# Attention of a two-block kernel: the softmax division moved from the probabilities to each head's output, with two units ahead

## The chip, the cores and the metric

The kernel runs on one core of one Trainium2 chip. The metric is the time of one execution in device microseconds (us); lower is better. The median of three runs stands for the kernel before.

## The reference, cut to what matters

Two transformer-like blocks work on one sequence of 1024 tokens of width 1024. The change lies in the attention of the second block: 8 heads of width 64, causal, with a bias of the distance and three dilated windows. Each branch is a softmax, and the three are merged by their softmax denominators:

```
for window, dilation in DILATED_BRANCHES:
    o, l = dilated_window_branch(q, k, v, slopes, window, dilation)
    ...
w = jax.nn.softmax(jnp.stack(lses, axis=-1), axis=-1)
o = jnp.einsum('bshn,nbshe->bshe', w, jnp.stack(outs, axis=0))
```

The merged branches equal one softmax over all keys, in which a key that lies in n branches counts n times. The kernel computes it so: the table `bias` of each head holds the distance term less log(n), and a large positive value where n is 0.

## The kernel before, in words

The kernel is one long program, traced by the class `Model`. Matrices are multiplied in two parts, a rounded high part and the rest (`hi`/`lo`, `wh`/`wl`, `ph`/`pl`), on TensorE. Tiles come from pools with a fixed number of buffers by tag: 32 buffers of 128x1024 floats with tag `u` (line 263), 5 of 128x512 for `tmp` (line 268), 8 PSUM banks (line 274), and 2 each of the tags `raw` and `xr` (line 305). Through `raw` go all weights on their way from DRAM: `fetch` (line 342) loads a piece into a `raw` buffer on SP's queue, ScalarE rounds it to `wh` (L351), GpSimd makes `wl` (L352); there are 5 buffers (`NW`) for the results, and a piece whose result has no buffer yet waits in `raw`.

Which instruction stands where in an engine's queue is not written by hand. Under `schedule_with_timeline_sim=True` a list scheduler goes through the traced program, simulates it with modelled durations and gives out buffers and places in the queues; among instructions that are ready the one earlier in the program goes first. On the chip each queue then runs in that fixed order.

The second block's mixer (`mixer2`, line 1655) makes q, k, v and u, runs the state-space part and its gate (`glu`, line 1507), and then `attention` (line 1634). What follows are four rounds of `down` (line 447) over the results of the gate and of the attention; each input is split by `hilo` (line 1499: ScalarE L1501, GpSimd L1504).

Attention goes through 8 heads in 4 pairs, and each head in 2 halves of 512 queries; a half is called a unit here, v0 to v15 in the order of the program. `heads_in` (line 1557) lays out the q and k of a pair: copies on ScalarE (L1565, L1566), subtractions on GpSimd (L1568, L1569), and DMAs on SP (L1567, L1570).

`softmax` (line 1582) takes a unit's 4 blocks of 128 queries. For each, TensorE makes the negated scores against all keys up to the block (L1601, L1602), VectorE adds the bias and takes the row minimum in one instruction (L1604), ScalarE makes the exponential in place and the row's sum, `den` (L1607), VectorE its reciprocal (L1608), and GpSimd multiplies the block of probabilities by it (L1609). A row is a partition here, so the reciprocal is one number a partition. An even unit (queries 0 to 511) has rows of 128 to 512 keys, an odd one of 640 to 1024.

`values` (line 1612) takes a unit's probabilities, 128 keys at a time: TensorE turns them (L1624), ScalarE rounds the result to `ph` (L1626), VectorE makes `pl` (L1627), and TensorE multiplies both by the head's values into the bank `po` (L1628, L1629). There queries run along the columns. At the end ScalarE copies one half of the bank to `vo` (L1631) and VectorE adds both halves into the pair's tile `at` (L1632).

`attention` keeps finished softmaxes in the list `late`. `values` of a unit is traced only after the softmax of the unit three later (line 1649).

Of the kernel before, what the change touches and what calls it, by code (L numbers as in the profile page):

```python
# [11 lines left out]
F32 = mybir.dt.float32  # L12
# [3 lines left out]
ALU = mybir.AluOpType  # L16
PSUM = bass.MemoryType.PSUM
DRAM = bass.MemoryType.DRAM
P = 128
# [3 lines left out]
H = 512  # L23
# [89 lines left out]
class Z:  # L113
# [3 lines left out]
    late = "s"  # L117
# [60 lines left out]
class ZS(Z):  # L178
# [4 lines left out]
    late = "u"  # L183
# [64 lines left out]
class Model:  # L248
# [1332 lines left out]

    def softmax(self, ops, bias, half):

        nc = self.nc
        qq, kd, kl = ops
        if half:
            ps = [self.u("P") for _ in range(4)]
        else:
            two = [self.u("P", shape=[P, 2, H]) for _ in range(2)]
            ps = [two[c // 2][:, c % 2] for c in range(4)]  # L1590
        mx, den = self.sm("mx", 8), self.sm("den", 4)
        for c, p in enumerate(ps):
            qb = 4 * half + c
            w = (qb + 1) * P
            o = 896 - qb * P
            cuts = [0, w] if w <= H else ([0, 384, w] if w < 896 else [0, H, w])
            init = 3.0e38
            for n, (k0, k1) in enumerate(zip(cuts, cuts[1:])):
                pp = self.bank()[:, : k1 - k0]
                qs = slice(qb * P, (qb + 1) * P)  # L1600
                nc.tensor.matmul(pp, qq[:, qs], kd[:, k0:k1], start=True, stop=False)  # L1601
                nc.tensor.matmul(pp, qq[:, qs], kl[:, k0:k1], start=False, stop=True)  # L1602
                m = mx[:, c : c + 1] if n == len(cuts) - 2 else mx[:, 4 + c : 5 + c]
                nc.vector.tensor_tensor_reduce(out=p[:, k0:k1], in0=pp, in1=bias[:, o + k0 : o + k1], scale=1.0,  # L1604
                                               scalar=init, op0=ALU.add, op1=ALU.min, accum_out=m)
                init = m
            nc.scalar.activation(p[:, :w], p[:, :w], AF.Exp, scale=-1.0, bias=mx[:, c : c + 1], accum_out=den[:, c : c + 1])  # L1607
            nc.vector.reciprocal(den[:, c : c + 1], den[:, c : c + 1])  # L1608
            nc.gpsimd.tensor_scalar(out=p[:, :w], in0=p[:, :w], scalar1=den[:, c : c + 1], scalar2=None, op0=ALU.mult)  # L1609
        return ps  # L1610

    def values(self, vv, a, ps, half, at):


        nc = self.nc
        po = self.bank("po")
        me, other = slice(64 * a, 64 * a + 64), slice(64 - 64 * a, 128 - 64 * a)
        last = 4 * half + 3
        for kt in range(last + 1):
            c0 = max(0, kt - 4 * half)  # L1620
            sl = slice(c0 * P, H)
            pp = self.bank()
            for c in range(c0, 4):
                nc.tensor.transpose(pp[:, c * P : (c + 1) * P], ps[c][:, kt * P : (kt + 1) * P], self.idn)  # L1624
            ph, pl = self.tmp("ph", dt=F32R), self.tmp("pl", dt=F32R)
            nc.scalar.activation(ph[:, sl], pp[:, sl], AF.Copy)  # L1626
            nc.vector.tensor_tensor(pl[:, sl], pp[:, sl], ph.bitcast(F32)[:, sl], op=ALU.subtract)  # L1627
            nc.tensor.matmul(po[:, sl], vv[:, kt, :], ph[:, sl], start=kt == 0, stop=False)  # L1628
            nc.tensor.matmul(po[:, sl], vv[:, kt, :], pl[:, sl], start=False, stop=kt == last)  # L1629
        t = self.tmp("vo")  # L1630
        nc.scalar.activation(t[me], po[other], AF.Copy)  # L1631
        nc.vector.tensor_tensor(at[me, half * H : half * H + H], po[me], t[me], op=ALU.add)  # L1632

    def attention(self, qk):

        at, late = [], []
        ops = [self.heads_in(*qk[0])]
        for j in range(4):
            at.append(self.u("at"))
            for a in range(2):  # L1640
                h = 2 * j + a
                bias = self.raw(self.a["bias"][h], name="bias", tag="xr")
                if a == 0 and j < 3:
                    ops.append(self.heads_in(*qk[j + 1]))
                vv = self.head_v(h)
                for half in range(2):
                    ps = self.softmax(ops[j][a], bias, half)
                    late.append((vv, a, ps, half, at[j]))
                    if len(late) > 3:
                        self.values(*late.pop(0))  # L1650
        while late:
            self.values(*late.pop(0))
        return [self.hilo(t) for t in at]
# [71 lines left out]
```

## Time and profile before

| | |
|---|---|
| median of 3 runs | 3072.33 us (3070.43 to 3072.90) |
| profiled execution, its own time | 3082.47 us |
| its span, first to last instruction | 3080.7 us |
| mean granted TensorE clock | 0.963 |
| busy, share of the span | TensorE 92%, VectorE 58%, ScalarE 43%, GpSimd 28% |
| chain that ended last | TensorE 62%, DMA 14%, VectorE 9%, ScalarE 6%, GpSimd 2% |
| attention in the span | about 2090 to 2270 us |

The profile shows one execution. PE is TensorE (PEld its weight loads), DVE VectorE, ACT ScalarE, POOL GpSimd and SP SyncE, which only issues DMAs here; L1609 is line 1609 of the kernel. Rows by line give busy time, mean ns of one, and the idle time of the engine just before them with what ended it. Rows in order of time give start and duration in us, and in brackets the idle time ahead. A release is inferred: with several waits it is the one that came last. Busy shares over the whole span are an average over stages with different limits.

### The profile page before, as it was taken

To read this page: it belongs to the slowest core of one execution; us is meant where nothing else is said; L and a number is where in the kernel's file an instruction comes from. 1 tells how busy PE (TensorE), PEld (TensorE's weight loads), DVE (VectorE), ACT (ScalarE), POOL (GpSimd) and SP (SyncE) were. 2 spreads that over 40 slices of the span, in tenths; PEclk is the share of its full clock that TensorE was granted. 3 is DMA by queue.
4 is the path that set the end of the run, shared out by engine and by line. 5 is a ranking of instruction groups with operands and counts; after the bars stand their busy time and mean duration, and the time that the engine had idled before them with its cause. 6 is when DMAs were issued, how large, how long until landed. Compare 5 with 4: busy or idle time off the path is not lost.

```text
span 3080.7 us, 33834 instructions
## 1 busy us (share of the span) xinstructions
PE 2821.6 (92%) x12585; PEld 2306.2 (75%) x12585; DVE 1775.9 (58%) x2527; ACT 1323.5 (43%) x1921; POOL 868.0 (28%) x667
## 2 busy tenths in 40 slices
PE   8998999898999979999978999997689899998998
PEld 7777788677777858777767778886677677776776
DVE  4576655487784365665667551417635756665445
ACT  5446555433445463333324452246644533333343
POOL 3331332211222432121111031459844212211002
PEclk9999999999999989999989999998899999999999
DMA  3114344564455123454466661523113244446556
GB/s 141 61 42 137 132 146 146 201 230 144 162 183 170 55 82 103 151 177 150 146 221 212 217 220 72 168 76 110 35 48 130 86 150 158 158 157 208 181 180 209
DMA packets 192309, 443.11 MB, mean 144 GB/s; under 512 B 23220, under 2 KB 23312, under 8 KB 192144
## 3 DMA queue, kind: packets, MB, share of 16 engines
q1 hardware_dynamic: 155600, 362.83, 35.4%
q10 hardware_dynamic: 36544, 78.13, 7.2%
q8 instruction: 98, 1.61, 0.2%
q14 instruction: 67, 0.55, 0.1%
HBM read 303.92 MB, written 131.60 MB: 141 GB/s over the span
## 4 chain that ended last, share of the span: by engine, by line
PE 62%; DMA 14%; DVE 9%; ACT 6%; issue 6%; POOL 2%; SPq 1%; ACTq 0%; DVEq 0%; POOLq 0%
PE b L541 22%; PE b L717 17%; PE b L455 4%; PE b L442 4%; DMA raw<-in_f_out 3%; DMA raw<-in_f_in 3%; DMA td<-tw 2%; DMA tw<-raw 2%; PE b L1103 2%; PE b L1101 2%; PE b L1102 2%; DMA sd<-hs 1%; ACT wh L481 1%; PE b L1624 1%; DVE wl L482 1%
## 5 line engine op out<-in xcount | busy, mean ns | idle before, releaser
L541 PE MATMUL b<-zh,wh 128*128 128x512 f32 x1680 | 644.9, 397 | 30.5 <-ACT wh L481 23.1
L541 PE MATMUL b<-zh,wl 128*128 128x512 f32 x1680 | 623.3, 392 | 8.4 <-DVE wl L482 3.3
L541 PE MATMUL b<-zl,wh 128*128 128x512 f32 x1560 | 612.8, 393 | 15.4 <-DVE zl L211 15.4
L717 PE MATMUL b<-tt,wh 128*128 128x512 f32 x1232 | 392.1, 400 | 51.8 <-ACT tt L698 46.5
L541 PEld LDWEIGHTS b<-zh,wh 128*128 128x128 f32 x1680 | 319.5, 190 | 117.2 <-ACT wh L481 35.1
L541 PEld LDWEIGHTS b<-zh,wl 128*128 128x128 f32 x1680 | 316.8, 189 | 78.6 <-DVE wl L482 4.6
L717 PE MATMUL b<-wl,wh 128*128 128x512 f32 x1344 | 323.5, 402 | 40.3 <-ACT wl L698 26.3
L541 PEld LDWEIGHTS b<-zl,wh 128*128 128x128 f32 x1560 | 295.4, 189 | 79.5 <-DVE zl L211 19.2
L717 PEld LDWEIGHTS b<-wl,wh 128*128 128x128 f32 x1344 | 258.7, 194 | 102.4 <-ACT wl L698 27.8
L717 PEld LDWEIGHTS b<-tt,wh 128*128 128x128 f32 x1232 | 237.5, 194 | 106.8 <-ACT tt L698 48.9
L482 POOL TENSOR_TENSOR wl<-raw,wh 128x1024 fp32r<-128x1024 f32 x60 | 148.0, 2469 | 392.4 <-ACT wh L481 368.9
L698 ACT ACTIVATE wh<-sd 128x1024 fp32r<-128x1024 f32 x140 | 141.7, 1014 | 254.3 <-PE b L717 127.0
L717 PE MATMUL b<-tt,wl 128*128 128x512 f32 x616 | 244.1, 397 | 0.0
L352 POOL TENSOR_TENSOR wl<-raw,wh 128x1024 fp32r<-128x1024 f32 (+1 forms) x58 | 142.6, 2464 | 305.0 <-ACT wh L351 274.1
L481 ACT ACTIVATE wh<-raw 128x1024 fp32r<-128x1024 f32 x120 | 126.8, 1059 | 226.0 <-DMA raw<-in_f_in 102.6
L383 POOL TENSOR_SCALAR v<-ss 128x1 f32<-128x1 f32 x80 | 46.4, 580 | 497.6 <-ACT junk L376 493.9
L618 POOL TENSOR_TENSOR hw<-h 128x512 f32<-128x512 f32 x38 | 59.2, 1558 | 409.2 <-DVE h L1188 173.2
L699 DVE TENSOR_TENSOR tt<-td,tt 128x1024 fp32r<-128x1024 f32 x84 | 95.2, 1134 | 115.4 <-ACT tt L698 115.2
L698 ACT ACTIVATE tt<-td 128x1024 fp32r<-128x1024 f32 x84 | 83.0, 988 | 162.7 <-DMA td<-tw 86.2
L699 DVE TENSOR_TENSOR wl<-sd,wh 128x1024 fp32r<-128x1024 f32 x84 | 97.4, 1159 | 77.1 <-ACT wh L698 77.1
L505 DVE TENSOR_TENSOR s<-raw 128x512 f32<-128x512 f32 x60 | 75.2, 1253 | 115.2 <-DMA raw<-in_f_in 105.2
L717 PEld LDWEIGHTS b<-tt,wl 128*128 128x128 f32 x616 | 119.1, 193 | 25.3
(362 smaller groups left out, 5301.0 us busy)
## 6 DMA issues: line engine op xcount, KB each, us to landing
sd<-hs SPq DMA_DIRECT2D x126, 512.0 KB, 4.0
raw<-in_f_in SPq DMA_DIRECT2D x94, 512.0 KB, 3.5
raw<-in_f_out SPq DMA_DIRECT2D x44, 512.0 KB, 3.6
tw<-raw SPq DMA_DIRECT2D x44, 512.0 KB, 2.9
wd<-in_w_down ACTq DMA_DIRECT2D x40, 512.0 KB, 8.9
td<-tw ACTq DMA_DIRECT2D x40, 512.0 KB, 4.3
hs<-h SPq DMA_DIRECT2D x38, 512.0 KB, 3.3
hs<-hw SPq DMA_DIRECT2D x38, 512.0 KB, 3.1
```

Source lines behind the costliest of these rows:

```text
L352: nc.gpsimd.tensor_tensor(l, r, h.bitcast(F32), op=ALU.subtract)
L442: nc.tensor.matmul(pp[n], w[:, k, :], z(m, k, slice(n * H, n * H + H)), start=k == 0 and w is wh and m == 0, stop=k == nk - 1 and w is wl)
L455: yield nc.tensor.matmul(pp, h[:, ts], w[:, sl], start=f == 0 and w is wh and h is hh, stop=f == len(hs) - 1 and h is hl)
L481: nc.scalar.activation(hi.rearrange("p a b -> p (a b)"), x, AF.Copy)
L482: eng.tensor_tensor(lo.rearrange("p a b -> p (a b)"), x, hi.bitcast(F32).rearrange("p a b -> p (a b)"), op=ALU.subtract)
L505: v.tensor_tensor(s1, a21, a22, op=ALU.add)
L541: self.mark = nc.tensor.matmul(bank, w, x, start=start and k == 0 and i == 0, stop=k == 3 and i == 2, skip_group_check=True)
L698: nc.scalar.activation(hi[:, :n], x[:, :n], AF.Copy)
L699: v.tensor_tensor(lo[:, :n], x[:, :n], hi.bitcast(F32)[:, :n], op=ALU.subtract)
L717: self.mark = nc.tensor.matmul(bank, x[:, c, ts], y[:, c], start=start and k == 0, stop=stop and k == 2, skip_group_check=True)
L1101: nc.tensor.matmul(pp, zh, wh[:, k % 2, :], start=k == 0, stop=False)
L1102: nc.tensor.matmul(pp, zh, wl[:, k % 2, :], start=False, stop=False)
```

## The change

Probabilities stay unscaled. After the 4 blocks of a unit one reciprocal covers the whole `den` tile (128x4). A DMA writes it transposed into a DRAM tile of 4x128, and a second DMA reads that row back as a broadcast to all 128 partitions, into one half of a tile `inv` that takes a buffer of the tag `raw` for a head. `values` adds the two halves of the bank into the temporary tile and multiplies that by `inv` into `at`. `values` of a unit is traced after the softmax of the unit two later.

```diff
@@ softmax
             nc.scalar.activation(p[:, :w], p[:, :w], AF.Exp, scale=-1.0, bias=mx[:, c : c + 1], accum_out=den[:, c : c + 1])
-            nc.vector.reciprocal(den[:, c : c + 1], den[:, c : c + 1])
-            nc.gpsimd.tensor_scalar(out=p[:, :w], in0=p[:, :w], scalar1=den[:, c : c + 1], scalar2=None, op0=ALU.mult)
-        return ps
-
-    def values(self, vv, a, ps, half, at):
+        nc.vector.reciprocal(den, den)
+        row = self.pd.tile([4, P], F32, name="den", tag="den", bufs=4)
+        if half == 0:
+            self.inv = self.pr.tile([P, 2, H], F32, name="inv", tag="raw")
+        inv = self.inv[:, half]
+        nc.sync.dma_start(out=row.rearrange("c q -> q c"), in_=den)
+        nc.sync.dma_start(out=inv, in_=row.rearrange("c q -> (c q)").partition_broadcast(P))
+        return ps, inv
+
+    def values(self, vv, a, ps, inv, half, at):
@@ values
         t = self.tmp("vo")
         nc.scalar.activation(t[me], po[other], AF.Copy)
-        nc.vector.tensor_tensor(at[me, half * H : half * H + H], po[me], t[me], op=ALU.add)
+        nc.vector.tensor_tensor(t[me], po[me], t[me], op=ALU.add)
+        nc.vector.tensor_tensor(at[me, half * H : half * H + H], t[me], inv[me], op=ALU.mult)
@@ attention
                 for half in range(2):
-                    ps = self.softmax(ops[j][a], bias, half)
-                    late.append((vv, a, ps, half, at[j]))
-                    if len(late) > 3:
+                    ps, inv = self.softmax(ops[j][a], bias, half)
+                    late.append((vv, a, ps, inv, half, at[j]))
+                    if len(late) > 2:
                         self.values(*late.pop(0))
```

## Rows read from the trace of the kernel before

**Rows 1.** Busy by stretch: from:to, length, PE, PEld, DVE, ACT, POOL (instructions), PE clock, DMA.

```profile
2090.00:2270.00 180.00, 129.83 (x671) 108.62 (x670) 125.01 (x378) 124.12 (x266) 144.18 (x79) 0.87 0.18 54
2098.00:2205.00 107.00, 75.96 (x383) 64.03 (x382) 74.23 (x244) 76.37 (x167) 105.83 (x58) 0.83 0.22 63
```

**Rows 2.** Groups of instructions by line, 2085 to 2270 us.

```profile
L1609 POOL TENSOR_SCALAR P<-P,den 128x640 f32<-128x640 f32 (+5 forms) x64 | 109.6, 1734 | 15.9 <-DVE den L1608 15.6
...
L1632 DVE TENSOR_TENSOR at<-po,vo 64x512 f32<-64x512 f32 x16 | 11.0, 688 | 10.4 <-ACT vo L1631 10.3
...
L1608 DVE RECIPROCAL den<-den 128x1 f32<-128x1 f32 x64 | 9.2, 154 | 8.1 <-ACT P L1607 7.9
...
L1565 ACT ACTIVATE qq<-qk 64x1024 fp32r<-64x1024 f32 x4 | 4.2, 1048 | 0.1
L1566 ACT ACTIVATE kd<-qk 64x1024 fp32r<-64x1024 f32 x4 | 4.2, 1040 | 0.0
```

**Rows 3.** Waits, 2085 to 2270 us: total us, times, longest us.

```profile
PE po L1628 <- ACT ph L1626: 36.7, 17, 7.8
...
PE b L1624 <- POOL P L1609: 6.5, 3, 3.7
```

**Rows 4.** VectorE in order of time, line L1632: ends of v0-v5, v7, v9, v12, v15.

```profile
2115.58 0.68 DVE L1632 TENSOR_TENSOR at<-po,vo 64x512 f32<-64x512 f32 x1 [1.27 <-ACT vo L1631]
...
2136.61 0.68 DVE L1632 TENSOR_TENSOR at<-po,vo 64x512 f32<-64x512 f32 x1
...
2141.95 0.69 DVE L1632 TENSOR_TENSOR at<-po,vo 64x512 f32<-64x512 f32 x1 [0.46 <-ACT vo L1631]
...
2153.06 0.69 DVE L1632 TENSOR_TENSOR at<-po,vo 64x512 f32<-64x512 f32 x1
...
2158.36 0.68 DVE L1632 TENSOR_TENSOR at<-po,vo 64x512 f32<-64x512 f32 x1 [1.33 <-ACT vo L1631]
...
2179.05 0.68 DVE L1632 TENSOR_TENSOR at<-po,vo 64x512 f32<-64x512 f32 x1
...
2196.32 0.69 DVE L1632 TENSOR_TENSOR at<-po,vo 64x512 f32<-64x512 f32 x1
...
2224.59 0.68 DVE L1632 TENSOR_TENSOR at<-po,vo 64x512 f32<-64x512 f32 x1
...
2246.59 0.68 DVE L1632 TENSOR_TENSOR at<-po,vo 64x512 f32<-64x512 f32 x1 [1.08 <-ACT vo L1631]
...
2268.23 0.69 DVE L1632 TENSOR_TENSOR at<-po,vo 64x512 f32<-64x512 f32 x1 [1.04 <-ACT vo L1631]
```

**Rows 5.** TensorE and ScalarE in order of time, at two of the stalls.

```profile
2119.59 0.48 PE L1624 MATMUL b<-idn,P 128*128 128x128 f32 x1 [3.71 <-POOL P L1609]
...
2158.16 1.04 ACT L1565 ACTIVATE qq<-qk 64x1024 fp32r<-64x1024 f32 x1
...
2165.68 0.79 PE L1628 MATMUL po<-ph,vv 128*128 128x512 f32 x1 [7.81 <-ACT ph L1626]
```

**Rows 6.** TensorE in order of time: the first scores, and the first transpose.

```profile
2089.77 0.22 PE L1601 MATMUL b<-kd,qq 128*128 128x128 f32 x1
...
2104.83 0.52 PE L1624 MATMUL b<-idn,P 128*128 128x128 f32 x3
```

**Rows 7.** DMAs, whole span: a queue's packets, MB, share; issues, KB, us to landing.

```profile
q1 hardware_dynamic: 155600, 362.83, 35.4%
...
g<-in_rows SPq DMA_DIRECT2D x3, 512.0 KB, 4.1
...
s5m<-kk SPq DMA_DIRECT2D x8, 4.0 KB, 2.8
```

**Rows 8.** Line L1521: duration ns min/median/max, first and last start us.

```profile
L1521 DVE TENSOR_TENSOR yt<-gs,yt x7: 679/2883/2891, 2077.5 to 2095.7; 128x512 f32<-128x512 f32 x7
```

**Rows 9.** In order of time: SP's last load in the stage, ScalarE's first rounding after it.

```profile
2105.97 0.33 SPq L307 DMA_DIRECT2D raw<-in_w_mo  x1
...
2293.42 1.06 ACT L351 ACTIVATE wh<-raw 128x1024 fp32r<-128x1024 f32 x1 [0.44 <-PE b L455]
```

## The prediction

> **What bounds the kernel now.** Over the whole run TensorE holds most of the chain of waits, so a change to another engine's work can pay only where TensorE stands still. The stage that the diff touches is therefore looked at alone, first as busy time by stretch. In the attention (2090 to 2270) nothing is full: TensorE 129.8 of 180 us, VectorE 125.0, ScalarE 124.1. Only GpSimd comes near, with 144.2, and from 2098 to 2205 it has 105.8 of 107 us [rows 1]. The groups by line say with what: the scaling of the probabilities in L1609 is 64 instructions, 109.6 us [rows 2]. The change takes exactly these out.
>
> A full engine off the matmul path need not bound anything, so the waits come next. TensorE waits for GpSimd by name only 6.5 us; it waits 36.7 us for ScalarE's copy `ph` (L1626) [rows 3]. The second could be the first in disguise. To see it, take the end of each unit (half a head; 16 of them, v0 to v15), which is its add in L1632 [rows 4]. Undisturbed, an even unit takes 5.3 us (v1 to v2) and an odd one 11.1 (v2 to v3), so 16.4 a head. Three places break this: v0 to v1 21.0 instead of 11.1 (9.9 too many), v4 to v5 20.7 (9.6), and v7 to v9 28.3 instead of 16.4 (11.9). Together 31.4 us.
>
> At the first of them TensorE waits 3.71 us for GpSimd's scaled P. At the second it waits 7.81 us for `ph`, while ScalarE is at the copies of the next pair of heads (L1565, L1566), which stand ahead of `ph` in its queue [rows 5]. Why there? The order on each engine is laid down beforehand by a list scheduler that simulates the kernel; I read it that GpSimd's backlog made these P's late in its plan, so that Exps and copies were put ahead of `ph`. That is an inference: the page shows orders, not the plan.
>
> **The change, part by part.** The sum is made against the profiled execution, 3082.5 us with a span of 3080.7; that stands 10.1 us over the median of 3072.3, and I carry the difference over to the median unchanged.
>
> 1. *L1609 goes.* GpSimd keeps 144.2 - 109.6 = 34.6 us of 180 and can bound nothing. Of the 31.4 us of stalls I keep the 8.4 us that the copies of two pairs cost ScalarE (4.2 + 4.2 [rows 2]), which must still be made somewhere, and drop 23.0. Bounds: everything goes, 31.4, or only the wait by name, 6.5. I take the value near the upper one, because undisturbed units show that the other engines hold 16.4 us a head. Late next would be ScalarE and VectorE, with some 125 and 135 us (part 4) of the 155 that remain.
>
> 2. *Two units ahead instead of three.* Before, four softmaxes run before the first transpose: 2104.8 - 2089.8 = 15.0 us, 3.8 each [rows 6]; at the end three units of values stand alone, v12 to v15, 21.6 us, 7.2 each [rows 4]. Each loses one unit, and one more runs jointly at 16.4/2 = 8.2. Saved: 3.8 + 7.2 - 8.2 = 2.8 us. P tiles held at once fall too, which lets `heads_in` start earlier; I price that at nothing.
>
> 3. *Reciprocals.* 64 of 0.154 become 16 of 128x4: nearest row the same 0.15, so VectorE loses 48 x 0.154 = 7.4 us of work, and 64 stops for an Exp become 16 [rows 2]. VectorE is not the bound: no time.
>
> 4. *The multiply by* `inv`. 16 new VectorE operations on 64x512 with both inputs in SBUF. The nearest row with such inputs is L1521, 128x512: 0.68 at least, 2.88 at the median, the slow ones while GpSimd works [rows 8]. GpSimd will work 34.6/180 = 19% of the stage, so 0.68 + 0.19 x 2.2 = 1.1 each, 17.6 in all; ends 10.9 and 46. With part 3 VectorE gets 125.0 + 17.6 - 7.4 = 135 us (ends 128 and 164): hidden below a stage of some 155. On the path lies only the last multiply, which the last `hilo` and with it the first matmul of `down` wait for: +0.7, and +1 for delays of VectorE's queue. This is where a rule speaks against the change. The Trainium skill (SBUF — State Buffer, section "SBUF: two separate sides") says that a VectorE instruction with two SBUF inputs and a GpSimd instruction that reads SBUF lock each other out for a whole instruction, where the old add, with one input in PSUM, was free of it. The trace agrees, 0.68 against 2.88; by the rule with GpSimd always at work it would be 46 us of VectorE, by the row and GpSimd's remaining share 17.6, and the sum is the same.
>
> 5. *Two DMAs a unit on SP's queue*, 32 in all, each an issue of 0.33 [rows 9], 10.6 us of a queue that has little else. The write W sends `den` to a transposed row: neighbouring values lie 512 bytes apart, so it falls into up to 512 pieces of 4 bytes. No row shows such a write. Lower bound: a small write, `s5m<-kk`, 2.8 us. Upper: 32 pieces on each of 16 DMA engines, at the mean time of a packet (35.4% x 16 x 3080.7 / 155600 = 0.112 us), 3.6 on top: 6.4. The read R is a broadcast of a row; the nearest is `g<-in_rows`, twice as large, 4.1; lower bound again 2.8 [rows 7]. I take W 4.6 (the middle, as neither row is near) and R 4.1. W + R + two issues is 9.4 us (6.3 to 11.2); between the last Exp of a unit and its multiply lie two units, 16.4. Hidden. Behind SP's wait for W stand R, the bias loads and the `kd`/`kl` copies of a later pair, needed a pair ahead: covered too. If the cover were gone, VectorE would stand at the multiply with all reductions and `pl` behind it.
>
> 6. *The buffer of* `inv` comes from the two `raw` buffers. Before, two pieces of `w_mo` sit in them for the whole stage: the last is loaded at 2106, and they are cast from 2293 on [rows 9]. If one stays, R of the next head starts only when the odd unit before is done, and its first use is an even unit later, 5.3 us; 4.1 + 0.33 fits. If both leave, their loads come after 2270 with 22 us of cover. Nothing either way; at worst 7 heads x (R at 6 us + 0.33 - 5.3) = 7 us.
>
> Sum: -23.0 - 2.8 + 0.7 + 1 = -24 us. 3082.5 becomes 3058.5 profiled, 3072.3 becomes **3048**.
>
> The Trainium skill (DMA: Bandwidth & Descriptors, section "Latency and other measured facts") also says that a strided last dimension becomes one descriptor per element. No run here shows it; it would put W at its upper bound of pieces, and the sum stays the same as long as W is hidden.
>
> **The rivals.** *Order, not GpSimd:* `ph` waits because Exps and copies are ahead of it, and they stay ahead. For it: the 7.81 us stall names ScalarE alone. Against: in undisturbed units the same Exps are there without a stall. Then only the 6.5 and the 2.8 go, and 1.7 is added: -8, 3064.
>
> *VectorE becomes the bound:* with the multiply at its slow end, 164 us of work, and the usual waits of its queue, the stage stays near 180: no change, 3072. Against: GpSimd is then 81% idle.
>
> *Slower: the row write paces.* SP keeps R behind the wait for W, and the next unit's W behind that, so a unit cannot be shorter than W + 0.7. This decides once that passes the old 180/16 = 11.3 us, so W over 10.6. At W = 12 the stage takes 16 x 12.7 = 203 us, +23: 3095. For it: 4-byte pieces occur nowhere in the trace. Against: my upper bound is 6.4.
>
> *It goes further:* all stalls vanish with the copies too, -31.4 - 2.8 + 1 = -33: 3039. This is the far end of my forecast, not a case of its own.
>
> **How the numbers follow.** The forecast, own range 3037 to 3059 (24 us with 11 more or less: some or all of the 8.4 us goes too, or as much again stays), has 0.69. Order has 0.15, VectorE 0.08, the slow write 0.08. The range of 8 in 10 runs from a little below the far end to past the order case: 3034 to 3068; it leaves out the last two cases and tails. 0.2% is 6 us, about what a measurement of this kernel can tell. Faster by more: 0.69, and 0.11 of the order case: 0.80. Within: the rest of it and VectorE, 0.12. Slower: 0.08.
>
> **What would show it.** Right: no L1609; GpSimd near 35 us in the stage; the steps between ends of units at 5 to 6 and 11 to 12 us throughout; waits for `ph` well below 36.7 us; TensorE's clock nearer 1 than 0.87; the multiply waiting for no DMA; the stage some 24 us shorter, and all after it only moved. Wrong: long steps that remain with ScalarE's Exps ahead of `ph` (order), VectorE above nine tenths (bound), or a multiply that waits for `inv` (write).

## The result, and the profile after

The changed kernel takes 3113.62 us (median of 4 runs, 3107.72 to 3116.57), the kernel before 3072.61 beside it: a ratio of 1.0127, 95% interval 1.0104 to 1.0150. It is slower by 41 us where I had forecast 24 us faster. The profiled execution has 3111.11 us and a span of 3109.2; the profiled execution of before lay 10 us above its median, so the two profiles differ by less (28.6 us) than the medians.

The lines of the profile move: the reciprocal is now L1609, the row write (W) L1614, the broadcast read (R) L1615, the transposes L1630, `ph` L1632, the products L1634 and L1635, the copy to `vo` L1637, the add L1638, the multiply L1639.

Below, the **stage** of a kernel is the time from the first score matmul to the first matmul of `down`. Before it ran from 2089.77 [rows 6] to 2271.08: 181.3 us. TensorE of the changed kernel in order of time:

```profile
2083.09 0.22 PE L1602 MATMUL b<-kd,qq 128*128 128x128 f32 x1
...
2296.87 1.22 PE L455 MATMUL b<-wh,hi 128*128 128x512 f32 x2 [4.17 <-ACT hi L1501]
```

The stage takes 213.8 us, 32.5 more. It also starts 6.7 us earlier; in the kernels below it starts anywhere from 2080.5 to 2090.3, and what sets that was not looked into. Busy time by stretch of the changed kernel (columns as in [rows 1]) says that no engine got much more to do:

```profile
2083.00:2295.00 212.00, 136.38 (x674) 109.65 (x672) 135.01 (x346) 122.56 (x265) 35.07 (x15) 0.83 0.37 63
```

GpSimd fell from 144.2 us to 35.1, as forecast, VectorE has the forecast 135, and TensorE's busy time is within some 7 us of what it was, over 32 us more. The DMA engines are busy 0.37 of the time instead of 0.18, at 63 GB/s instead of 54. So everything waits more. The waits of the changed kernel from 2085 to 2300 (total us, times, longest) name SP's queue; the first row is SP's own, the others those of the engines:

```profile
SPq L1615 <- DMA den<-den: 151.6, 16, 11.4
```

```profile
PE po L1634 <- ACT ph L1632: 43.3, 18, 21.2
...
ACT wh L351 <- DMA raw<-in_w_mo: 25.3, 2, 19.6
...
DVE at L1639 <- DMA inv<-den: 14.4, 4, 5.5
```

TensorE's wait for `ph` went up from 36.7 [rows 3] to 43.3 instead of well down; 21.2 us of it are one wait, which comes up again below. SP stands for 151.6 us of the stage waiting for row writes to land. The DMAs of the same stretch (KB each, median us to landing):

```profile
inv<-den SPq DMA_DIRECT2D x16, 256.0 KB, 5.1
bias<-in_bias SPq DMA_DIRECT2D x6, 512.0 KB, 8.2
...
den<-den SPq DMA_DIRECT2D x16, 2.0 KB, 11.1
```

Two kilobytes take 11.1 us, twice as long as the 256 KB of the broadcast. SP in order of time shows what follows from that:

```profile
2102.60 1.43 SPq L1614 DMA_DIRECT2D den<-den  x2
2113.71 1.03 SPq L1615 DMA_DIRECT2D inv<-den  x2
...
2239.84 0.32 SPq L1615 DMA_DIRECT2D inv<-den  x1
...
2240.68 0.42 SPq L1614 DMA_DIRECT2D den<-den  x1
2251.83 0.32 SPq L1615 DMA_DIRECT2D inv<-den  x1
2252.25 0.38 SPq L1614 DMA_DIRECT2D den<-den  x1
2262.74 0.32 SPq L1615 DMA_DIRECT2D inv<-den  x1
...
2263.59 0.42 SPq L1614 DMA_DIRECT2D den<-den  x1
2275.30 0.32 SPq L1615 DMA_DIRECT2D inv<-den  x1
2275.76 19.38 SPq L307 DMA_DIRECT2D raw<-in_w_mo  x4
```

R stands behind the landing of W, and the next W goes out only behind that R. The one exception is the second and the third W, which went out together (2102.60) and landed together: their Rs follow at 2113.71. So from the first W (2093.01) to the last R (2275.30) the 182.3 us are 15 such turns, 12.2 us each. These two writes, under way at once, landed 11.1 and 11.3 us after their issue, as one alone does. So much of the pace lies in the order W, R, W, R of the queue; what it would be with every W ahead of the R before it was not tried. And four loads of `w_mo`, of which the last went out at 2105.97 before [rows 9], now stand behind the last R, because `inv` took the `raw` buffers that they sit in. ScalarE, and TensorE behind it, pay for that near the end; the rows are ScalarE's and TensorE's in order of time:

```profile
2281.83 1.06 ACT L351 ACTIVATE wh<-raw 128x1024 fp32r<-128x1024 f32 x1 [19.58 <-DMA raw<-in_w_mo]
...
2284.17 0.79 PE L1634 MATMUL po<-ph,vv 128*128 128x512 f32 x1 [21.17 <-ACT ph L1632]
```

The rounding of a weight stands ahead of v14's and v15's copies in ScalarE's queue. So the trace alone offers two culprits, the pace of the writes and the late weight, and says nothing yet of the parts that were meant to gain.

### The profile page after: what moved, and what is told of

The parts are those of the page before. It is cut to its first block, busy times and chain, and to the rows that moved or that the text cites. A ratio compares the mean times of both kernels' runs of the same rounds, so it can differ in the third digit from the quotient of the medians.

```text
span 3109.2 us, 33738 instructions
## 1 busy us (share of the span) xinstructions
PE 2835.8 (91%) x12585; PEld 2312.6 (74%) x12585; DVE 1783.6 (57%) x2495; ACT 1324.1 (43%) x1921; POOL 761.3 (24%) x603
## 2 busy tenths in 40 slices
DMA packets 203060, 447.33 MB, mean 144 GB/s; under 512 B 31924, under 2 KB 32016, under 8 KB 202896
## 4 chain that ended last, share of the span: by engine, by line
PE 60%; DMA 16%; DVE 10%; ACT 6%; issue 5%; POOL 2%; SPq 1%; ACTq 0%; DVEq 0%; POOLq 0%
PE b L541 22%; PE b L717 18%; PE b L455 4%; PE b L442 3%; DMA raw<-in_f_out 3%; DMA raw<-in_f_in 2%; DMA td<-tw 2%; DMA den<-den 2%; PE b L1103 2%; PE b L1101 2%; PE b L1102 2%; DMA tw<-raw 2%; DMA sd<-hs 1%; ACT wh L481 1%; DMA raw<-in_w_up 1%
## 5 line engine op out<-in xcount | busy, mean ns | idle before, releaser
L717 PEld LDWEIGHTS b<-wl,wh 128*128 128x128 f32 x1344 | 258.2, 194 | 102.2 <-ACT wl L698 28.6
L351 ACT ACTIVATE wh<-raw 128x1024 fp32r<-128x1024 f32 (+1 forms) x58 | 59.5, 1030 | 192.9 <-issue 42.7
```

What stands on the lines that cost most here:

```text
L717: self.mark = nc.tensor.matmul(bank, x[:, c, ts], y[:, c], start=start and k == 0, stop=stop and k == 2, skip_group_check=True)
```

## The experiments

All ratios are to the kernel before, run beside it on the same chip, with 95% intervals. The median of the kernel before was 3078.46 us beside runs 1 to 4, 3077.41 beside runs 5 to 8 and 3079.98 beside runs 9 to 12.

**1. The changed kernel without the trip through DRAM.** What is left is the end of GpSimd's scaling, the extra multiply, and two units ahead. The division is left out.

```diff
-        row = ...; inv = ...
-        nc.sync.dma_start(out=row.rearrange("c q -> q c"), in_=den)
-        nc.sync.dma_start(out=inv, in_=...)
-        nc.vector.tensor_tensor(at[...], t[me], inv[me], op=ALU.mult)
+        nc.vector.tensor_tensor(at[...], t[me], t[me], op=ALU.mult)
```

> This kernel is the changed one without the row: no write of den, no inv, no read; the multiply takes the sum with itself, so the division is left out. Theory 'trip' (the write of 512 pieces holds SP's queue, and through it the multiplies and the late loads of w_mo): the whole loss goes and the forecast gain appears, 3045 to 3055 us. Rival 'order' (two units ahead and the scheduler's order starve TensorE, the trip is a bystander): it stays at or above the kernel before, 3075 to 3115. Rival 'GpSimd was no bound': about as before, 3068 to 3076, since the scaling that went was hidden.

Measured: 3069.81 us, ratio 0.9966 (0.9953 to 0.9978); stage 173.3 us. So the trip costs 213.8 - 173.3 = 40.5 us of the stage, more than the whole loss. But without it only 8.0 us of the stage are gained, a third of my 24: something else is wrong too. The time is above the 3045 to 3055 of the theory 'trip' and falls into the range of the rival 'GpSimd was no bound', which run 5 takes up.

**2. The trip with the row in the other order.** The row is written as it lies in `den`, queries outermost: 128 pieces of 16 bytes instead of 512 of 4. The multiply reads `inv` with a stride.

```diff
-        row = self.pd.tile([4, P], F32, ...)
-        nc.sync.dma_start(out=row.rearrange("c q -> q c"), in_=den)
+        row = self.pd.tile([P, 4], F32, ...)
+        nc.sync.dma_start(out=row, in_=den)
...
+        inv[me].rearrange("p (q c) -> p c q", c=4)
```

> The row is kept in the order in which den lies in SBUF (128 pieces of 16 bytes for the write instead of 512 of 4), read back as one run, and the multiply reads inv with a stride. Theory 'pieces' (the write's time goes with its number of pieces): it lands in about a third to a half, 4 to 5 us, SP's waits fall from 152 to about 70 us, and the time to 3045 to 3060. Rival 'latency' (a trip through DRAM costs so much whatever its pieces): the write still lands in 9 to 11 us and the time stays at 3100 to 3115. Rival 'order': the write gets fast and the time stays above 3075.

Measured: 3078.03 us, ratio 0.9999 (0.9988 to 1.0011); stage 176.3. Its row write in the profile:

```profile
den<-den SPq DMA_DIRECT2D x16, 2.0 KB, 1.4
```

The same 2 KB to the same place land in 1.4 us instead of 11.1, and 37.5 of the 40.5 us are gone. R, the queue's order and the buffers of `raw` are all still there (the extra multiply stands in run 1 as well), so next to the size of the pieces they cost little. The time still stays above 3075 us, as the rival 'order' had it.

**3. Two units ahead alone, and 4. three units ahead in the changed kernel.** One number in the kernel before, and in the changed one.

```diff
-                    if len(late) > 3:      (3: kernel before)
+                    if len(late) > 2:
-                    if len(late) > 2:      (4: changed kernel)
+                    if len(late) > 3:
```

> The kernel before with values two units behind instead of three and nothing else: the probabilities are still scaled by GpSimd. Forecast of my sum: 2.8 us less from a shorter run-in and run-out, if GpSimd's backlog has the same room; 3068 to 3072. Rival 'order': the shorter distance by itself costs, because the scaled P's come later than their transposes: 3080 to 3115.

> The changed kernel with three units ahead again. Theory 'trip': the multiplies get a unit more of cover, so their 14 us of waits go, but SP's queue is still paced by 16 writes of 11 us and w_mo still stands behind the last read: 3090 to 3110. Rival 'two units are too few': back to 3050 to 3075.

Measured: run 3 took 3089.17 us, ratio 1.0036 (1.0023 to 1.0049), stage 189.3; run 4 took 3098.56 us, ratio 1.0062 (1.0039 to 1.0085), stage 199.0. Two units ahead, which I had at a gain of 2.8 us, costs 8.0 us of the stage in one kernel, as the rival 'order' had it, and 213.8 - 199.0 = 14.8 in the other. The trip with its 4-byte pieces costs as much under three units: W 10.6 us there.

**5. Three units ahead without the trip, and 6. three units ahead with the other order of the row.** Runs 1 and 2 with the edit of run 4.

> As the run without the trip (no write, no inv, no read; the multiply takes the sum with itself, the division is left out), but with values three units behind again. It completes the square of scaling by GpSimd yes or no and two or three units. Theory 'distance costs' (two units behind cost some 10 us with or without GpSimd's scaling, as the kernel before with two units did, +0.36%): 3050 to 3062 us, so about 20 us below the kernel before. Theory 'GpSimd was hardly the bound': 3066 to 3074, the same as with two units.

> The row in the order of den (128 pieces) and values three units behind: the candidate for the best. Theory 'distance costs': its trip is as cheap as with two units (the write lands in about 1.4 us) and the distance gives back some 10 us: 3055 to 3068, faster than the kernel before. Rival 'distance is nothing once the trip is short': 3074 to 3082, as with two units.

Measured: run 5 (division left out) took 3056.97 us, ratio 0.9938 (0.9922 to 0.9953), stage 158.1. Run 6 computes all of the reference and took 3062.16 us, ratio **0.9955** (0.9942 to 0.9967), stage 166.2: it beats the kernel before and the changed one. The stages together, in us:

| units ahead | GpSimd scales | no scaling, no trip | trip, 16-byte pieces | trip, 4-byte pieces |
|---|---|---|---|---|
| three | 181.3 (before) | 158.1 (5) | 166.2 (6) | 199.0 (4) |
| two | 189.3 (3) | 173.3 (1) | 176.3 (2) | 213.8 (changed) |

With three units ahead the trip in 16-byte pieces costs 166.2 - 158.1 = 8.1 us of the stage, where it cost 3.0 with two. The ratios follow the stages: 158.1 is 23.2 us under 181.3, and 0.62% of 3077 us is 19; 199.0 is 17.7 over it, and 0.62% is again 19.

Busy time by stretch of run 5 shows what the end of L1609 gave (columns as in [rows 1]):

```profile
2085.00:2235.00 150.00, 115.12 (x652) 92.83 (x652) 124.73 (x339) 117.87 (x261) 31.93 (x14) 0.98 0.20 60
```

VectorE is now the fullest, with 124.7 of 150 us; the granted clock is 0.98 of full speed where it was 0.87 with the stalls. The ends of its units and the copies `ph` show where two units ahead lose. ScalarE in order of time (the copy to `vo` of a unit is its end; L1631 and L1626 in these two kernels), run 5, three ahead, v4 to v5:

```profile
2142.18 0.59 ACT L1631 ACTIVATE vo<-po 64x512 f32<-64x512 f32 x1 [1.53 <-PE po L1629]
2142.80 0.60 ACT L1626 ACTIVATE ph<-b 128x512 fp32r<-128x512 f32 x1
...
2145.19 0.58 ACT L1626 ACTIVATE ph<-b 128x512 fp32r<-128x512 f32 x1
...
2147.82 0.60 ACT L1626 ACTIVATE ph<-b 128x512 fp32r<-128x512 f32 x1
...
2148.97 0.39 ACT L1608 ACTIVATE P<-P,mx 128x128 f32<-128x128 f32 x1
...
2156.18 0.59 ACT L1631 ACTIVATE vo<-po 64x512 f32<-64x512 f32 x1
```

And run 1, two ahead, the same step, with some of what stands between:

```profile
2150.10 0.59 ACT L1631 ACTIVATE vo<-po 64x512 f32<-64x512 f32 x1 [1.64 <-PE po L1629]
...
2153.36 0.60 ACT L1626 ACTIVATE ph<-b 128x512 fp32r<-128x512 f32 x1 [0.77 <-PE b L1624]
2153.98 1.06 ACT L1565 ACTIVATE qq<-qk 64x1024 fp32r<-64x1024 f32 x1
...
2156.84 0.92 ACT L1608 ACTIVATE P<-P,mx 128x768 f32<-128x768 f32 x1
...
2157.76 0.57 ACT L1626 ACTIVATE ph<-b 128x512 fp32r<-128x512 f32 x1
2158.23 1.03 ACT L1608 ACTIVATE P<-P,mx 128x896 f32<-128x896 f32 x1
...
2159.78 1.14 ACT L1608 ACTIVATE P<-P,mx 128x1024 f32<-128x1024 f32 x1
...
2160.91 0.58 ACT L1626 ACTIVATE ph<-b 128x512 fp32r<-128x512 f32 x1
...
2168.30 0.59 ACT L1631 ACTIVATE vo<-po 64x512 f32<-64x512 f32 x1 [0.75 <-PE po L1629]
```

The step takes 18.2 us with two ahead and 14.0 with three. The first three `ph` copies are spread over 7.6 us (2153.36 to 2160.91) instead of 5.0, and between them stand the Exps of an odd unit, 640 to 1024 keys wide, beside the copies of the next pair. In the whole step ScalarE makes the four Exps of v7 (odd) and the four of v8 with two ahead, and the four of v8 and two of v9 with three. Over the whole stage the steps that end at v1, v5, v9 and v13 lose 4.3 + 4.2 + 2.6 + 4.7 = 15.8 us that way, and the others 4.5.

The same step in the kernel before, ScalarE in order of time, shows what GpSimd's scaling had done there:

```profile
2162.73 0.39 ACT L1607 ACTIVATE P<-P,mx 128x128 f32<-128x128 f32 x1
...
2164.20 0.71 ACT L1607 ACTIVATE P<-P,mx 128x512 f32<-128x512 f32 x1
...
2165.03 0.60 ACT L1626 ACTIVATE ph<-b 128x512 fp32r<-128x512 f32 x1
```

There the copies of the next pair (from 2158.16 [rows 5]) and all four Exps of v8 come first, and the first `ph` only behind them, 7.4 us after the copy to `vo` of v4 (2157.66). In run 5 the same copies and Exps are made, but the first `ph` comes at once, and two more come before the first Exp.

**7. The pace or the late weight.** In the changed kernel `inv` takes a buffer of the tag `u` instead of `raw`, so that `w_mo` keeps its buffers.

```diff
-            self.inv = self.pr.tile([P, 2, H], F32, name="inv", tag="raw")
+            self.inv = self.u("inv", shape=[P, 2, H])
```

> The changed kernel with one edit: inv takes a buffer of the tag u instead of raw, so the loads of w_mo need not wait behind the last inv. Theory 'w_mo behind the last read': ScalarE's stop of 19.6 us at the rounding of w_mo near the end goes, and with it about 20 us: 3088 to 3098. Rival 'pacing alone': the time is set by 16 writes of 11 us one after another and stays at 3108 to 3118.

Measured: 3109.60 us, ratio 1.0109 (1.0095 to 1.0123); stage 212.7. The waits of VectorE and ScalarE in that stage:

```profile
DVE at L1639 <- DMA inv<-den: 32.9, 8, 7.2
...
ACT wh L351 <- DMA raw<-in_w_mo: 7.0, 2, 5.5
```

The stall of 19.6 us for the weight is gone, and the time is where it was: VectorE now waits 32.9 us for `inv` instead of 14.4, SP 165.0 us for W instead of 151.6, and the last R goes out at 2289.34 instead of 2275.30. But the chain of writes got longer with it: from the first W (2094.22) to the last R are 195.1 us instead of 182.3. A turn is as long as before, 12.2 us, but no two Ws went out together here, so there are 16 turns instead of 15. So the run tells that freeing the `raw` buffers wins nothing back; it does not hold the pace still, and so does not price the late weight alone. An estimate of that: `down` starts 7.7 us after the last R goes out in run 7, and 21.6 in the changed kernel, so some 14 us of the changed kernel's stage may lie with the weight.

**8 to 10. What makes the write slow.** In three kernels with two units ahead and without R and `inv` (the division is left out), the same 512 pieces of 4 bytes are written 512 bytes apart (8), side by side as in the change (9), and 64 bytes apart (10).

```diff
         (8: z = 128, 10: z = 16; 9 keeps the row of the change)
+        row = self.pd.tile([4, P, z], F32, ...)
+        nc.sync.dma_start(out=row[:, :, 0:1].rearrange("c q z -> q c z"), in_=den.unsqueeze(2))
```

> Without read and inv (the division is left out as in the run without the trip), but den is written in 512 pieces of 4 bytes, each into a block of 512 bytes of its own. It measures the write alone. Theory 'number of pieces': it lands in 10 to 12 us as the packed write does, 0.3 us for each of the 32 pieces of a DMA engine. Rival 'pieces of one block collide' (neighbouring values, from different engines, go into the same block): it lands in 2 to 5 us.

> The changed kernel with its row write as it is (512 neighbouring pieces of 4 bytes), but with no read back and no tile for it; the multiply takes the sum with itself, so the division is left out. Control for the spread row. Theory (neighbouring pieces hold each other up): the write lands in 10 to 12 us here too, as in the changed kernel (11.1), and the time is 3065 to 3080 because nothing waits for it. Rival (it is the broadcast read of the unit before that slows the write): without reads the write lands in 1.5 to 4 us, as the spread row did (1.8).

> The same without the read back, with each 4-byte piece at the start of a 64-byte place of its own (512 pieces, 32 KB between the first and the last; division left out). Theory A (pieces collide when they fall into one 64-byte block): 1.5 to 2.5 us from issue to landing, as with 512-byte places (1.8). Theory B (they collide in a larger block, 512 bytes or so): with 8 pieces in such a block in place of 128, still 4 to 11 us. The time stays at 3065 to 3080 either way.

Measured, the row write of each in its profile, 8, 9 and 10 in turn:

```profile
den<-den SPq DMA_DIRECT2D x16, 2.0 KB, 1.8
```

```profile
den<-den SPq DMA_DIRECT2D x16, 2.0 KB, 8.7
```

```profile
den<-den SPq DMA_DIRECT2D x16, 2.0 KB, 1.9
```

512 pieces are no trouble by themselves: 1.8 us, below even my lower bound of 2.8. Neighbouring ones are: 8.7 us without any read in the stage, and 64 bytes of distance are enough to end it. The control came out below the 10 to 12 I had expected, so some 2 us of the 11.1 come from what else moves in the changed kernel. R is one such thing: by the trace's records of DMA packets, the pieces of the changed kernel's W of 2154.05, issued 0.4 us behind an R, move from 3.2 to 4.2 us after its issue, those of run 9's W of 2146.29 from 0.9 to 1.3. Nothing waits for these writes, and the three single times (3069.28, 3077.43 and 3076.15 us) are not above the kernel before.

Nor is it the moving of the pieces that takes long. Run 9's W of 2146.29 lands at 2154.77; the stretches are around the moving of its pieces and from there to the landing. The third is of the changed kernel, ahead of the landing of its W of 2154.05 at 2165.49 (columns as in [rows 1], the DMA engines' share last but one):

```profile
2147.10:2147.60 0.50, 0.26 (x1) 0.26 (x2) 0.47 (x2) 0.19 (x1) 0.00 (x0) 1.00 0.51 4
2147.60:2154.70 7.10, 5.75 (x34) 4.57 (x33) 4.80 (x12) 3.53 (x6) 1.47 (x1) 1.00 0.00 0
```

```profile
2158.30:2165.40 7.10, 5.08 (x17) 3.93 (x18) 6.17 (x16) 5.53 (x15) 1.58 (x1) 0.76 0.03 1
```

In run 8, too, the pieces of a W move from 0.9 to 1.3 us after its issue, and it lands half a microsecond later. With neighbouring pieces some 7 us pass in which the DMA engines show next to no packets and the write has not landed. What goes on in them, no trace here shows.

The Trainium skill (DMA: Bandwidth & Descriptors, section "Specifications") says that below 512 bytes a DMA engine reads, modifies and writes back. Whether it is this that makes neighbours wait, no run here shows. Nor do the runs tell how large the block is within which pieces hold each other up: if 128 pieces in 512 bytes took 8.7 us one after the other, the 8 pieces that run 10 has in 512 bytes would take 0.5 and be hidden in its 1.9. They show that 64 bytes of distance are enough, and that 16-byte pieces side by side are not held up.

**11. The write on another queue.** The changed kernel with W issued by GpSimd, R by SP.

```diff
-        nc.sync.dma_start(out=row.rearrange("c q -> q c"), in_=den)
+        nc.gpsimd.dma_start(out=row.rearrange("c q -> q c"), in_=den)
```

> The changed kernel with one edit: the packed row write is issued on GpSimd's queue instead of SP's; the read stays on SP. Theory (the write's own time is what matters and SP's queue adds the strict alternation of write and read, some 11.4 + 5.1 us for a unit): with the writes on another queue the next write no longer stands behind the read before it, so the pace falls towards the write's own time; ratio 1.000 to 1.008, SP's wait for the write still 80 us or more in the stage. Rival (the queue is no part of it, only the write's latency against the cover of two units): ratio 1.010 to 1.015, as the changed kernel (1.0127).

Measured: 3109.05 us, ratio 1.0097 (1.0077 to 1.0117); stage 210.4, W 10.8 us. Between the two forecasts, and nearer the rival's. GpSimd in order of time says why so little came of it:

```profile
2173.70 0.77 POOL L1614 DMA_DIRECT2D den<-den  x1 [0.29 <-DVE vo L1638]
2184.74 0.76 POOL L1614 DMA_DIRECT2D den<-den  x1 [10.27 <-DVE pl L1633]
2195.28 0.75 POOL L1614 DMA_DIRECT2D den<-den  x1 [9.78 <-DVE pl L1633]
2206.68 0.76 POOL L1614 DMA_DIRECT2D den<-den  x1 [10.64 <-DVE pl L1633]
```

The writes still go out one after the other, 10.5 to 11.4 us apart, about the 10.8 that one takes. (The releasers in brackets had long been done; each write goes out about 0.3 us after the landing of the one before, as the Rs that wait for these landings show, which SP issues at 2184.45, 2195.03 and 2206.39. Why GpSimd's queue waits for it, the trace does not tell.) From the first W (2095.96) to the last R (2274.47) are 16 turns of 11.2 us, where SP's queue had 12.2: the other queue saves a microsecond a turn, and what is left is the write's own time, still one write after the other. The Trainium skill (DMA: Bandwidth & Descriptors, section "Issuing engines are not separate DMA queues") says that DMAs run on the same engines whoever issues them and that another issuer saves only issue time; this run agrees, 210.4 us of stage against 213.8.

**12. Four units ahead** in run 6's kernel (`len(late) > 4`).

> The row written with queries outermost, 16-byte pieces (as in the run with three units ahead, ratio 0.9955), with values four units behind their softmax. Theory (each unit ahead buys cover against uneven even and odd units; two to three bought 0.4%): gain falling off, ratio 0.992 to 0.9965. Rival (more unscaled probabilities held at once use up the buffers of tag u, and the last four units of values stand alone): ratio 0.998 to 1.004.

Measured: 3083.49 us, ratio 1.0018 (1.0006 to 1.0031); stage 181.7, against 166.2 with three and 176.3 with two. The rival won. Three is not one point on a slope but the best of the three values. With three ahead the values of a long unit meet the softmax of a short one; with two or four, long meets long. The traces bear that out: in the step v4 to v5 ScalarE makes all four Exps of v7 in runs 1, 2 and 3 and all four of v9 in run 12, beside the four of v8 or v10; in runs 5 and 6 it makes the four of v8 and only two of v9. But with four the buffers of the tag `u` may get scarce as well, and no run tells the two apart.

## Why the prediction was wrong, step by step

**Part 1, GpSimd's scaling: right in kind and size.** I had -23.0 us, on the inference that `ph` was late because of GpSimd's backlog in the scheduler's plan. With three units ahead, taking L1609 out made the stage 181.3 - 158.1 = 23.2 us shorter (run 5), though it was never more than 6.5 us of wait by name [rows 3]. By the copies to `vo`, the steps v0 to v1 and v4 to v5 are 14.0 instead of 20.0 and 19.1 and v7 to v9 17.6 instead of 27.7: the three places that the prediction named give 21.2 of the 23.2 us. TensorE's wait for `ph` falls from 36.7 us, with 7.8 the longest, to 25.9, with 1.6 the longest, and `ph` no longer stands behind the copies and Exps in ScalarE's queue. The rival "order, not GpSimd" (a gain of 6.5) falls. What no run parts from L1609 is part 3: run 5 also has 16 reciprocals instead of 64, and the extra multiply.

**Part 2, two units ahead instead of three: this step failed, with the wrong sign.** I had -2.8 us, from the ends of the stage alone: a shorter lead-in, a shorter tail, one more joint unit. The lead-in did get shorter, 19.0 us to the first end of a unit in run 1 against 24.1 in run 5, 5.1 where I had 3.8 for it. What I left out is that the number also decides which softmax runs beside which values in all the units between: +20.3 us from v0 to v15. In sum +15.2 without the trip, +8.0 in the kernel before.

**Parts 3 and 4, reciprocal and multiply: held.** The multiply in the changed kernel, by line:

```profile
L1639 DVE TENSOR_TENSOR at<-vo,inv 64x512 f32<-64x512 f32 x16 | 14.5, 906 | 14.7 <-DMA inv<-den 14.4
```

0.91 us each, 14.5 in all, where I took 1.1 and 17.6; its shortest is 0.67 and its longest 2.45, as the row L1521 had it [rows 8]. VectorE's 135.0 us is the forecast, in part by luck: the multiply came out 3.1 us cheaper, the reciprocals saved 6.4 us (16 of 0.175) instead of 7.4, and by these the sum would be 133.1; the stretch is also 32 us longer. That the reciprocals save no time was not tested apart. What the row adds is the idle time behind the bar, which belongs to part 5.

**Part 5, the two DMAs: this step failed.** "I take W 4.6", "Upper: 32 pieces on each of 16 DMA engines, at the mean time of a packet", 6.4 us. The bound took pieces to run on 16 engines at a mean packet's price, whatever they fall on. Measured were 1.8 us where they lie apart and 11.1 where they touch, and most of the 11.1 passes after the pieces have moved, in a wait for the landing that the bound did not have (runs 8 and 9). So a bound from a mean over packets of other sizes and places was no bound, and I had written myself that no row shows such a write. R was sized well enough, 5.1 against 4.1. W, R and two issues are then 16.9 us, already past the 16.4 of cover. The rule of the Trainium skill (DMA: Bandwidth & Descriptors) cited there, one descriptor for each element of a strided last dimension, stands in its section "Rules for kernel authors", not in the one named. It is seen: packets under 512 bytes in the whole span rise by 31924 - 23220 = 8704, which are 16 writes of 512 pieces, 8192, and 16 packets of 4 bytes for each of the 32 new transfers. In the prediction it stood as harmless while W is hidden.

The rival "the row write paces" told the mechanism as it came, but for the one pair of Ws: R behind W, the next W behind R. Its threshold was still too high. It compared W + 0.7 with 181 / 16 = 11.3 us, which holds the lead-in and the tail of the stage, as if they too were paced. Without the trip a unit takes 9.9 us (v1 to v13 of run 1: 118.5 / 12), so the write decides from W = 9.2 on, not 10.6. Against run 1, the 40.5 us of the trip in the changed kernel are, by the ends of units: +5.8 at v0 to v1, +14.6 from v1 to v13, +20.5 from v13 to v15, where the late weight stands, -0.4 before v0.

**Part 6, the buffer of** `inv`**: wrong in place, but not what sets the pace.** I had the loads of `w_mo` after the stage "with 22 us of cover". They went out at 2275.76, and the scheduler had put the rounding of the first one ahead of v14's end: 19.6 us of wait. Run 7 took that wait away and gained no more than the intervals leave open (1.0109 against 1.0127), while its chain of writes took a turn more. So in the changed kernel some 14 us may lie here (the estimate of run 7), and without the slow writes little does: run 2 has its `inv` in the `raw` buffers too, and its whole trip costs 3.0 us.

So the sum of the stage reads -23.2 (part 1, with parts 3 and 4 in it) + 15.2 (part 2) + 40.5 (part 5, with part 6 in it) = 32.5 us, where I had -23 - 2.8 + 1.7 + 0.

## What to carry to other kernels

Before a small write to DRAM is taken as hidden, look at what its pieces fall on: neighbouring 4-byte pieces can cost eight times as much as the same bytes in 16-byte pieces, and a cheap reordering (write in the order of the source, stride the reader) avoids it. A DMA that waits for another on the same queue makes the pair a pacemaker as soon as the next pair stands behind it, and its period is to be held against the bare step of the loop, not against the stage with its ends. The number of units that run ahead is not a buffer depth alone; where units differ in length it decides which ones meet, so it is tried on its own.

## What the runs showed of the hardware that was not expected

- 512 pieces of 4 bytes from SBUF to DRAM land in 1.8 us when they lie 512 bytes apart, in 1.9 at 64 bytes, and in 8.7 to 11.1 side by side; 128 pieces of 16 bytes, side by side in the same 2 KB, in 1.4 us (2.5 in run 6).
- A write of 512 pieces side by side (run 9, issued at 2146.29) lands after 8.5 us, but its packets have ended 1.3 us after the issue; in between the DMA engines show none for 7.1 us.
- Two of these writes issued 0.5 us apart on SP's queue landed after 11.1 and 11.3 us (changed kernel, 2102.60), and a pair 0.7 us apart after 14.6 and 14.0 (run 9, 2104.97), where one alone took some 8 to 9 in run 9.
- Issued by GpSimd, the same write is counted as 32 packets instead of 528 (512 packets on that queue for 16 writes in the stage) and takes 10.8 us all the same. The packet count of a queue does not tell this cost.
- While the slow writes ran, other transfers were late too: the bias loads of 512 KB took 8.2 us at the median instead of 3.2, the `kl` copies of 256 KB 11.3 instead of 4.4.
